# Later first casts, a later store and a later turn of the stream in the two MLPs of a hybrid decoder trunk

## Chip, cores and metric

One core of a Trainium2 chip runs the whole kernel. The metric is the device time of one launch in microseconds (us), the median of three runs. A profiled execution of the same program gives the rows below; its span runs from the first to the last instruction.

## What is computed

The reference is a decoder trunk of two layers on a stream x of 512 tokens with 1024 features, all in float32. Each layer adds an attention block and then an MLP to the stream. Cut to what matters here:

```
x = x + mixer(rms_norm(x, g_mix))                    # attention, one kind per layer
x = x + square(relu(rms_norm(x, g_ffn) @ w_up)) @ w_down
```

`w_up` is 1024 x 4096 and `w_down` 4096 x 1024. After layer 0 a shared compressed key/value is computed from the stream; after layer 1 a last RMS norm ends the trunk.

## The kernel before

Every float32 product is made of three TensorE matmuls: each operand is cut into a rounded part ("hi") and the rest ("lo"), and `three` (line 238) multiplies hi by hi, hi by lo and lo by hi. For a weight tile this costs a **cast** on ScalarE (`w_cast`, line 673) and a **low** subtraction on VectorE (`w_low`, line 683). The activations are cut the same way in `scaled` (line 260). The gain of the norm is multiplied in there; the norm's factor per token is computed apart and multiplied in at the end.

An MLP (`ffn`, line 631) is a list `seq` of products, one per step. The first eight steps are up products U0 to U7 (`up_mm`, line 709: 24 matmuls of 512 columns each into one bank of PSUM); from step 8 on up products alternate with down products (q1, q5, p6, x3 and so on). The up products have two PSUM banks (tag "up"). A bank comes free when `up_post` (line 721) has read it on ScalarE, so U2 cannot begin before `up_post(0)` has read U0.

The order of the work around a product is written by hand. `at(step, rank, fn)` (line 662) puts a piece of work into `due`; steps are emitted in order, and within one step by rank: 0 the product itself, 1 `up_post` of the product before, 3 a low, 6 a cast, 9 a load. While this runs (`order["on"]`, line 866) every instruction on TensorE, VectorE and ScalarE is chained to the one emitted before it on the same engine (lines 109 to 121), so that each of these three engines keeps the written order. SyncE, which issues the loads, is not chained: a scheduler at compile time places its instructions, and may issue a load earlier than written. Work emitted before the steps (the out projection, `scaled`, the store and the turn below) isn't chained either.

For the up product of step m the piece of weights is loaded at step m-8 (512 KB, line 700), cast at step m-5 and given its low at step m-4 (lines 840 to 842); steps below -8 count as -8. The raw pieces have only two buffers, so load 3 waits until the low of piece 1 has been taken, load 4 until that of piece 2, and so on. The weights of the down products come as "quads" (`quad`, line 702, 512 KB each), which have eight buffers of their own. The number of a cast, low or load below is that of its up product. Piece 0 is loaded and cut during the out projection.

Two things stand in step 0 beside U0. Behind its matmuls `rstd_of` (line 275) sums the squares on TensorE and starts the norm's factor: three short VectorE instructions (lines 286 to 289), then twelve on GpSimd. They have rank 0, being part of `up_mm(0)`. In layer 0 `rstd_tile` follows U2 (line 719): TensorE spreads the factor along the tokens and ScalarE copies it.

Before the steps of the MLP of layer 0 the stream (`x`, eight tiles of 256 KB) is stored to DRAM (lines 876 and 877), to be read again at its end. Before those of layer 1 `turn_stream` (line 1132) turns the stream into rows of tokens: 32 transposes on TensorE in eight units of four, and eight copies on ScalarE.

Of the kernel before, what the change touches and what calls it, by code (L numbers as in the profile page):

```python
# [17 lines left out]
P = 128  # L18
D = 1024
S = 512  # L20
NB = S // P
KD = D // P
# [31 lines left out]

PATTERN = "U U q1 U q5 U p6 U x3 U x2 U x4 U p7".split()
CLOSING_PATTERN = "U U q1 U U q5 U p6 U U x3 U x2 p7 x4".split()
V4_BEFORE = (5, 6)


# [13 lines left out]
def pieces():  # L73
# [3 lines left out]
    for p in range(1, FH // 2):  # L77
        out += [("v4", 1024)] * (2 * V4_BEFORE.count(p)) + [("qk", 1024)] * 2
    out += [("fo", 1024)] * 8
# [15 lines left out]
@with_exitstack  # L95
def trunk(ctx: ExitStack, tc: tile.TileContext, xT, wts, gains, fing, rope, out):
    real = tc.nc
    order = {"on": False, "last": {}}

    class Engine:  # L100

# [4 lines left out]
        def __getattr__(self, op):  # L106
            fn = getattr(self.engine, op)

            def call(*args, **kw):
                ins = fn(*args, **kw)  # L110
                if order["on"]:
                    before = order["last"].get(self.name)
                    if before is not None:
                        tc.add_manual_dep(
                            ins.ins,
                            before,
                            mybir.DependencyInfo(mybir.DependencyClass.NoSync, mybir.DependencyReason.DATA),
                            reason="as written",
                        )
                    order["last"][self.name] = ins.ins.name  # L120
                return ins

            return call

    class Core:
        tensor, vector, scalar = (Engine(n) for n in ("tensor", "vector", "scalar"))
        sync, gpsimd = real.sync, real.gpsimd

    nc = Core()

# [5 lines left out]
    keep = ctx.enter_context(tc.tile_pool(name="keep", bufs=1, space=bass.MemoryType.DRAM))  # L136
# [13 lines left out]
    def nm(s):  # L150
        uid[0] += 1
        return f"{s}{uid[0]}"

    def bank(tag, shape=(P, S)):
        return psum["pool"].tile(list(shape), F32, tag=tag, name=nm(tag), bufs=psum["tags"][tag])

    def rt(shape=(P, S)):
        return rp.tile(list(shape), F32R, tag="r", name=nm("r"))
# [4 lines left out]
    def f32(ap):  # L163
        return ap.bitcast(F32)
# [8 lines left out]
    ident = const.tile([P, P], F32, name="ident")  # L173
# [86 lines left out]
    def scaled(x, gname, k):  # L260
        hi, lo = rt(), rt()
        nc.scalar.activation(out=hi, in_=x, func=AF.Copy, scale=g(gname, k))
        nc.vector.scalar_tensor_tensor(out=lo, in0=x, scalar=g(gname, k), in1=f32(hi), op0=ALU.mult, op1=ALU.subtract)
        return hi, lo
# [162 lines left out]
    with ExitStack() as fx:  # L427
# [16 lines left out]
        acc = xs[0]  # L444
# [63 lines left out]
        for kp in range(4):  # L508
            whi, wlo = piece("v")
            for tb in range(NB):  # L510
                for k2 in range(2):
                    k = kp * 2 + k2
# [10 lines left out]
        def v4_gen(q):  # L523
            ws = [piece("v4"), piece("v4")]
            for tb in range(NB):
                pp = bank("acc")[:, :256]
                t = slice(tb * P, (tb + 1) * P)
                for k in range(KD):
                    whi, wlo = ws[k // 4]
                    c = slice(k % 4 * 256, k % 4 * 256 + 256)  # L530
                    three(pp, whi[:, c], wlo[:, c], h[k][0][:, t], h[k][1][:, t], k == 0, k == KD - 1, flip=True)
                    if k == 3:
                        yield 6
                value_parts(q, tb, pp)
                yield 6
# [54 lines left out]
        for p in range(1, FH // 2):  # L590
            for q in range(2):
                if V4_BEFORE[q] == p:
                    fill.add(("v4", q + 2), v4_gen(q + 2))
# [16 lines left out]
    def out_proj(name, ctxs, res, outs):  # L610

        acc = tt()
        for f in range(KD):
            xf = f32(rt())
            nc.sync.dma_start(xf, res[:, f, :])
            if f < len(outs):
                op, w = outs[f]
                three(op, *w[KD - 1], *ctxs[KD - 1], False, True)
            else:
                op = bank("acc")  # L620
                linear(op, piece(name), ctxs)
            nc.vector.tensor_tensor(xf, xf, op, op=ALU.add)
            square_sum(acc, xf, f == 0)
            x.append(xf)
        return acc

    x = []
    acc = out_proj("fo", [parts[k] for k in range(KD)], xT, outs)


    def ffn(acc, layer, tokens, tail, begin=None):

# [5 lines left out]
        with ExitStack() as fs:  # L640
            rawp = fs.enter_context(tc.tile_pool(name="mlp_raw", bufs=8, reuse_waits="tile"))
            sp = fs.enter_context(tc.tile_pool(name="mlp_s", bufs=4, reuse_waits="tile"))
            h = [scaled(x[k], gname, k) for k in range(KD)]
            if begin:
                begin()
            s, quads, s1, held, filled = {}, {}, {}, {}, set()
            norm = {}

# [2 lines left out]
            for c in range(CHUNKS):  # L651
                n = 8 * (c + 1)
                for what in CLOSING_PATTERN if c == CHUNKS - 1 else PATTERN:
                    if what == "U":
# [7 lines left out]
            def at(step, rank, fn, *args):  # L662
                due.setdefault(max(step, -8), []).append((rank, len(due.get(max(step, -8), [])), fn, args))
# [70 lines left out]
            def right(hf, kind):  # L734
                q = {f"B{a + 1}{b + 1}": quads.get((hf, a, b)) for a in range(2) for b in range(2)}
                return q["B11" if kind in ("T1", "T2", "T4") else "B12" if kind == "T3" else kind]
# [95 lines left out]
            for m, (what, n) in enumerate(seq):  # L832
                own = m % 2 == 0
                if what == "U":
                    if n == 0:
                        parts_ = state["ready"].pop(first)
                        los[0] = [tuple(t[:, j * S : (j + 1) * S] for t in parts_) for j in range(2)]
                    else:
                        src = lambda i=first + n: raws[i]
                        at(m - 8, 9, load, first + n)  # L840
                        at(m - 5, 6, w_cast, m, src, own)
                        at(m - 4, 3, w_low, m, src)
                    at(m, 0, up_mm, m, n)
                    at(m + 1, 1, up_post, n)
                    continue
                lk, rk = PRODUCTS[what]
                ready = max(posted[4 * n + j] for j in range(4))
                for key in {"q1": ["00"], "q5": ["01"], "p6": ["11"], "x2": ["10"]}.get(what, []):
                    at(m - 10, 9, quad, n, int(key[0]), int(key[1]))
                if rk[0] == "T":  # L850
                    at(m - 6, 4, right_sum, n, rk)
                if lk[0] == "S":
                    assert ready <= m - 4
                    at(max(m - 6, ready), 4.5, left_sum, n, lk)
                src = lambda n=n, rk=rk: right(n, rk)
                at(m - 5, 6, w_cast, m, src, own)
                at(m - 4, 3, w_low, m, src)
                assert ready <= m - 3
                at(max(m - 4, ready), 5, s_cast, m, n, lk)
                at(max(m - 3, ready + 1), 2, s_low, m, n, lk)  # L860
                at(m, 0, down_mm, m, what, n)
                if n % 2 and what[0] != "p":
                    at(m + 1, 1, down_post, what)
            tail(len(seq), max(posted.values()), at, locals())
            for step in sorted(due):
                order["on"] = True
                for _, _, fn, args in sorted(due[step], key=lambda d: d[:2]):
                    fn(*args)
            order["on"] = False
# [3 lines left out]

    stage("mlp0", up=2, go=2, keep=4)
    xmid = keep.tile([P, KD, S], F32, name="xmid")
    for k in range(KD):
        nc.sync.dma_start(xmid[:, k, :], x[k])
    xkeep = keep.tile([P, KD, S], F32, name="xkeep")
    ytok = [[f32(rt()) for _ in range(2)] for _ in range(NB)]
    xnew, hk, hm = {}, {}, {}  # L880
# [66 lines left out]
            for b in range(2):  # L947
                at(e + j // 2, 4, combine, b, part)

    ffn(acc, 0, ytok, by_features)  # L950
    for f in range(4, KD):
        close_feature(f)
    acc = closing["acc"]
# [10 lines left out]
    with ExitStack() as mx:  # L964
# [44 lines left out]
        for part in range(2):  # L1009
            for n in range(3):  # L1010
                w = blocks(piece("ka"))
                for m in range(2):
                    q = 2 * n + m
                    for j in range(4):
                        k = 4 * part + j
# [104 lines left out]
    x = []  # L1120
    acc = out_proj("mo", ctxs, xkeep, outs)
# [4 lines left out]
    xtok = [[f32(rt()) for _ in range(2)] for _ in range(NB)]  # L1126
# [2 lines left out]
    nc.scalar.dma_start(gfin, fing.partition_broadcast(P))  # L1129
    sums = fpool.tile([P, 2, NB], F32, name="sums")  # L1130

    def turn_stream():
        for tb in range(NB):
            for o in range(2):
                pp = bank("keep")
                for j in range(4):
                    nc.tensor.transpose(pp[:, j * P : (j + 1) * P], x[4 * o + j][:, tb * P : (tb + 1) * P], ident)
                nc.scalar.copy(xtok[tb][o], pp)

    def half_sum(tb, o):  # L1140
        junk = tt()
# [75 lines left out]
def _cols(w, lo, n):  # L1217
    return _blk(w, slice(lo, lo + n))


def _pack(i):
# [7 lines left out]
    for p in range(1, 8):  # L1229
        for q in range(2):  # L1230
            if V4_BEFORE[q] == p:
                b = _cols(fw, 2 * W + (q + 2) * 256, 256)
# [82 lines left out]
```

## Time and profile before

| | us |
|---|---|
| median of three runs | 1160.76 |
| the three runs | 1160.25, 1160.76, 1166.07 |
| the profiled execution's own time | 1166.28 |
| its span | 1164.5 |
| TensorE matmul busy in the span | 1128.8 |

The span is 1.8 us shorter than the profiled execution's own time. The MLP of layer 0 begins at about 262 us of the span and that of layer 1 at about 808 us. Nearly every instruction carries line 110, the helper that chains the engines, so groups are told apart by tiles: `up` is the bank of an up product, `go` that of the norm's sums, `keep` that of a transpose, `raw` a loaded piece of up weights, `q` a quad, `rs` the norm's factor, `s` the output of `up_post`, `whi`, `wlo` and `r` cut weights or activations. "[5.58 <-ACT s]" behind an instruction says that its engine was idle for 5.58 us before it and that an instruction of ScalarE writing `s` ended this.

### The profile page before, as it was taken

The page shows a single profiled execution, that of the slowest core. Times are in us where ns is not written, and L with a number is a line of the kernel's source. Part 1 is how long each engine was busy: PE and PEld are TensorE (multiplying, and loading weights), DVE is VectorE, ACT ScalarE, POOL GpSimd, SP SyncE. Part 2 cuts the span into 40 slices and gives each one's busy share as a digit, 9 for nine tenths or more (in the row PEclk, how much of TensorE's full clock was granted, in tenths as well). Part 3 has the DMA queues.
Part 4 walks back from the last instruction along what each step waited for, and adds up shares of the span by engine and source line. Part 5 has one row for each costly group of instructions (what it writes and reads, how often), then busy time and mean ns, then how long its engine had stood idle before and what let it go on. Part 6 is the DMA issues. An engine that isn't in the chain of part 4 may idle for free.

```text
span 1164.5 us, 14272 instructions
## 1 busy us (share of the span) xinstructions
PE 1128.8 (97%) x5356; PEld 922.3 (79%) x5356; DVE 783.0 (67%) x1413; ACT 574.4 (49%) x1053; POOL 22.4 (2%) x86
## 2 busy tenths in 40 slices
PE   8999999997999999999999899999899999999996
PEld 6777887786888888888887768788688888888875
DVE  6797888773457676677893678836346666765775
ACT  5555655554455454444353466626446444445611
POOL 1000000001000000000000100000100000000000
PEclk9999999998999999999999889999899999999998
DMA  5422222185204315211342121315511512511301
GB/s 184 128 101 80 74 91 73 37 281 206 73 37 154 99 43 192 74 55 64 119 167 91 34 64 50 109 55 191 189 37 54 181 57 71 184 64 41 127 1 73
DMA packets 36565, 116.65 MB, mean 100 GB/s; under 512 B 4224, under 2 KB 4864, under 8 KB 36496
## 3 DMA queue, kind: packets, MB, share of 16 engines
q1 hardware_dynamic: 35888, 114.15, 30.0%
q8 instruction: 42, 0.69, 0.3%
q0 software_dynamic: 320, 1.05, 0.2%
q10 hardware_dynamic: 288, 0.55, 0.2%
q14 instruction: 27, 0.22, 0.1%
HBM read 109.40 MB, written 6.32 MB: 99 GB/s over the span
## 4 chain that ended last, share of the span: by engine, by line
PE 90%; DMA 3%; DVE 3%; ACT 2%; issue 1%; POOL 1%; SPq 0%; POOLq 0%; ACTq 0%
PE up L110 32%; PE acc L110 20%; PE go L110 17%; PE sc L110 8%; PE tp L110 7%; PE keep L110 6%; DMA raw<-wts 2%; DVE r L110 1%; ACT r L110 1%; DVE wlo L110 1%; DMA q<-wts 1%; DMA nb<-csc 0%; DMA t<-xT 0%; DVE t L110 0%; DVE sl L110 0%
## 5 line engine op out<-in xcount | busy, mean ns | idle before, releaser
L110 PE MATMUL acc<-r,whi 128*128 128x512 f32 x600 | 196.2, 407 | 5.3 <-ACT whi L110 4.9
L110 PE MATMUL up<-r,r 128*128 128x512 f32 x808 | 192.4, 390 | 1.2 <-ACT s L110 1.2
L110 PE MATMUL up<-r,whi 128*128 128x512 f32 x544 | 173.7, 396 | 10.2 <-ACT s L110 10.2
L110 PEld LDWEIGHTS up<-r,r 128*128 128x128 f32 x808 | 151.4, 188 | 33.1 <-ACT s L110 1.4
L110 DVE TENSOR_TENSOR t<-s,t 128x512 fp32r<-128x512 f32 x84 | 57.8, 688 | 128.8 <-ACT t L110 128.7
L110 DVE TENSOR_TENSOR wlo<-raw,whi 128x1024 fp32r<-128x1024 f32 (+3 forms) x95 | 111.3, 1171 | 42.5 <-ACT whi L110 42.3
L110 ACT CAST whi<-raw 128x1024 fp32r<-128x1024 f32 (+3 forms) x95 | 95.5, 1008 | 86.6 <-PE acc L110 28.7
L110 PEld LDWEIGHTS acc<-r,whi 128*128 128x128 f32 x600 | 111.2, 192 | 31.1 <-ACT whi L110 4.9
L110 ACT ACTIVATE s<-up 128x512 f32<-128x512 f32 x56 | 33.4, 597 | 198.3 <-PE up L110 198.3
L110 PEld LDWEIGHTS up<-r,whi 128*128 128x128 f32 x544 | 103.7, 191 | 32.5 <-ACT s L110 11.1
L110 PE MATMUL acc<-r,wlo 128*128 128x512 f32 x300 | 119.2, 397 | 0.0
L110 PE MATMUL up<-r,wlo 128*128 128x512 f32 x288 | 113.3, 393 | 0.0
L110 PE MATMUL go<-r,t 128*128 128x512 f32 x360 | 86.5, 389 | 0.0
L110 PE MATMUL sc<-r,r 128*128 128x512 f32 (+6 forms) x480 | 81.5, 360 | 2.0 <-ACT r L110 1.6
L110 PE MATMUL go<-whi,t 128*128 128x512 f32 x240 | 78.7, 389 | 0.0
L110 PEld LDWEIGHTS go<-r,t 128*128 128x128 f32 x360 | 67.6, 188 | 14.0
L110 PEld LDWEIGHTS sc<-r,r 64*128 64x128 f32 (+1 forms) x480 | 55.9, 188 | 25.8 <-issue 10.3
L110 ACT ACTIVATE t<-t,sm 128x512 f32<-128x512 f32 (+3 forms) x96 | 53.3, 557 | 36.7 <-DVE sm L110 36.2
L110 DVE TENSOR_TENSOR r<-raw,r 128x512 fp32r<-128x512 f32 x72 | 46.5, 685 | 33.9 <-ACT r L110 33.9
L110 PEld LDWEIGHTS acc<-r,wlo 128*128 128x128 f32 x300 | 57.4, 191 | 12.8 <-issue 0.4
L110 DVE TENSOR_TENSOR wlo<-q,whi 128x1024 fp32r<-128x1024 f32 x45 | 54.9, 1221 | 16.7 <-ACT whi L110 16.3
L110 PEld LDWEIGHTS up<-r,wlo 128*128 128x128 f32 x288 | 55.0, 191 | 11.6
(180 smaller groups left out, 1869.4 us busy)
## 6 DMA issues: line engine op xcount, KB each, us to landing
raw<-wts SPq DMA_DIRECT2D x122, 512.0 KB, 3.5
q<-wts SPq DMA_DIRECT2D x56, 512.0 KB, 4.5
nb<-csc SPq DMA_DIRECT2D x8, 512.0 KB, 4.8
t<-xT SPq DMA_DIRECT2D x8, 256.0 KB, 5.9
r<-xT SPq DMA_DIRECT2D x8, 256.0 KB, 5.6
xmid<-r SPq DMA_DIRECT2D x8, 256.0 KB, 5.4
r<-xmid SPq DMA_DIRECT2D x8, 256.0 KB, 4.4
xkeep<-r SPq DMA_DIRECT2D x8, 256.0 KB, 2.3
```

The lines of the kernel that those rows point to most:

```text
L110: ins = fn(*args, **kw)
```

## The change

Three edits. The casts of the up products of steps 1 to 9 move to later steps by the table `BEGIN`: for m = 1 to 9 the cast stands at steps -1, -1, 0, 1, 2, 3, 4, 4, 5 (before: -4, -3, -2, -1, 0, 1, 2, 3, 4), and each low one step after its cast. The store of the stream in layer 0 moves into steps 1 to 4 (two tiles each, rank 9.5, behind the loads of the step). The turn of layer 1 moves into steps 1 to 8 (one unit each behind the step's product, its copy one step later). SyncE is chained in the written order for all steps below 9.

```
+BEGIN = (0, -1, -1, 0, 1, 2, 3, 4, 4, 5)
...
-                if order["on"]:
+                if order["on"] and (self.name != "sync" or order["loads"]):
...
-        tensor, vector, scalar = (Engine(n) for n in ("tensor", "vector", "scalar"))
-        sync, gpsimd = real.sync, real.gpsimd
+        tensor, vector, scalar, sync = (Engine(n) for n in ("tensor", "vector", "scalar", "sync"))
+        gpsimd = real.gpsimd
...
-            if begin:
-                begin()
...
+                        cast = max(m - 5, min(m - 2, BEGIN[m])) if m < len(BEGIN) else m - 5
                         at(m - 8, 9, load, first + n)
-                        at(m - 5, 6, w_cast, m, src, own)
-                        at(m - 4, 3, w_low, m, src)
+                        at(cast, 6, w_cast, m, src, own)
+                        at(cast + 1, 3, w_low, m, src)
...
+            begin(at)
             tail(len(seq), max(posted.values()), at, locals())
             for step in sorted(due):
-                order["on"] = True
+                order["on"], order["loads"] = True, step < 9
...
-    for k in range(KD):
-        nc.sync.dma_start(xmid[:, k, :], x[k])
+    def put_away(at):
+        for k in range(KD):
+            at(1 + k // 2, 9.5, lambda k: nc.sync.dma_start(xmid[:, k, :], xold[k]), k)
...
-    def turn_stream():
-        for tb in range(NB):
-            for o in range(2):
-                pp = bank("keep")
...
+    def turn_stream(at):
+        turned = {}
...
+        for n, (o, tb) in enumerate((o, tb) for o in range(2) for tb in range(NB)):
+            at(1 + n, 0.5, turn, tb, o)
+            at(2 + n, 1.5, lambda tb, o: nc.scalar.copy(xtok[tb][o], turned[tb, o]), tb, o)
```

## Rows read from the trace of the kernel before

**Rows 1.** The page's first part: busy time, share and instructions of each engine.
```profile
PE 1128.8 (97%) x5356; PEld 922.3 (79%) x5356; DVE 783.0 (67%) x1413; ACT 574.4 (49%) x1053; POOL 22.4 (2%) x86
```

**Rows 2.** Busy time by stretch, layer 0: length, engines, granted clock, DMA share, GB/s.
```profile
274.20:279.80 5.60, 0.03 (x1) 0.03 (x1) 2.90 (x7) 2.29 (x5) 3.85 (x12) 0.69 0.56 186
279.80:283.30 3.50, 3.50 (x9) 2.78 (x10) 1.45 (x2) 1.62 (x2) 0.48 (x2) 0.52 0.56 155
...
287.00:289.20 2.20, 1.02 (x10) 0.83 (x8) 0.00 (x0) 1.17 (x3) 0.00 (x0) 1.00 0.00 0
```

**Rows 3.** The same view, beginning of the MLP of layer 1.
```profile
823.50:828.10 4.60, 0.02 (x1) 0.02 (x1) 1.05 (x3) 1.67 (x4) 2.02 (x11) 0.76 0.58 214
```

**Rows 4.** Timeline of TensorE, layer 0: start, duration, instruction, idle before.
```profile
267.63 0.95 PE L110 MATMUL go<-ones,t 128*128 128x1 f32 x8
268.44 5.75 PE L110 MATMUL up<-r,r 128*128 128x512 f32 x24
279.77 1.22 PE L110 MATMUL up<-r,whi 128*128 128x512 f32 x2 [5.58 <-ACT s L110]
...
286.91 1.05 PE L110 MATMUL go<-ident,rs 128*128 128x128 f32 x8
289.13 5.74 PE L110 MATMUL up<-r,r 128*128 128x512 f32 x24 [1.18 <-ACT s L110]
```

**Rows 5.** Timeline of TensorE, beginning of the MLP of layer 1.
```profile
807.65 2.15 PE L110 MATMUL keep<-ident,r 128*128 128x128 f32 x16
...
810.58 1.91 PE L110 MATMUL keep<-ident,r 128*128 128x128 f32 x16
...
828.08 1.22 PE L110 MATMUL up<-r,whi 128*128 128x512 f32 x2 [4.63 <-ACT s L110]
...
835.78 5.60 PE L110 MATMUL up<-r,r 128*128 128x512 f32 x24
```

**Rows 6.** The chain that ended last, layer 0: start, duration, what.
```profile
266.38 6.09 DMA raw<-wts
...
273.19 1.29 DVE r L110 x2
...
274.51 3.55 DMA raw<-wts
...
278.08 1.14 ACT r L110 x2
```

**Rows 7.** The same chain at the beginning of the MLP of layer 1.
```profile
815.57 3.70 DMA raw<-wts
...
821.27 5.11 DMA raw<-wts
```

**Rows 8.** The chain of the whole span: an up product in the steady stretch.
```profile
332.95 5.44 PE up L110 x24
```

**Rows 9.** Timeline of VectorE, layer 0: the start of the norm's factor.
```profile
274.40 0.15 DVE L110 TENSOR_SCALAR rs<-go 128x4 f32<-128x4 f32 x1
274.59 0.38 DVE L110 TENSOR_SCALAR rs<-rs 128x4 int32<-128x4 int32 x2
```

**Rows 10.** Busy time by stretch: while load 3 was under way, and a steady stretch.
```profile
264.00:270.40 6.40, 6.40 (x34) 5.41 (x33) 3.57 (x5) 2.44 (x4) 0.00 (x0) 1.00 1.01 394
...
300.00:320.00 20.00, 20.00 (x90) 16.57 (x89) 9.25 (x12) 9.90 (x16) 0.00 (x0) 1.00 0.14 45
```

**Rows 11.** Timelines of ScalarE and VectorE, layer 1: copies of the turn, last low activations.
```profile
809.73 3.97 ACT L110 COPY r<-keep 128x512 f32<-128x512 f32 x8
...
809.86 0.75 DVE L110 SCALAR_TENSOR_TENSOR r<-r,gsb,r 128x512 fp32r<-128x512 f32 x1
```

**Rows 12.** TensorE in the attention of layer 1: a stop, and the stretch after it.
```profile
676.93 0.73 PE L110 MATMUL sc<-r,r 128*128 128x512 f32 x2 [1.26 <-ACT r L110]
...
678.00:680.00 2.00, 2.00 (x6) 0.92 (x6) 0.98 (x3) 1.80 (x4) 0.00 (x0) 0.77 0.78 222
```

More of the change, by code (lines that the diff above doesn't have):

```diff
@@ L97, in trunk @@
     real = tc.nc
-    order = {"on": False, "last": {}}
+    order = {"on": False, "loads": False, "last": {}}
     class Engine:
@@ L628, in trunk, with ffn @@
     acc = out_proj("fo", [parts[k] for k in range(KD)], xT, outs)
-    def ffn(acc, layer, tokens, tail, begin=None):
+    def ffn(acc, layer, tokens, tail, begin):
         gname = f"ffn{layer}"
@@ L875, in trunk @@
     xmid = keep.tile([P, KD, S], F32, name="xmid")
-    for k in range(KD):
-        nc.sync.dma_start(xmid[:, k, :], x[k])
+    xold = x
+    def put_away(at):
+        for k in range(KD):
+            at(1 + k // 2, 9.5, lambda k: nc.sync.dma_start(xmid[:, k, :], xold[k]), k)
     xkeep = keep.tile([P, KD, S], F32, name="xkeep")
@@ L948, in by_features @@
                 at(e + j // 2, 4, combine, b, part)
-    ffn(acc, 0, ytok, by_features)
+    ffn(acc, 0, ytok, by_features, put_away)
     for f in range(4, KD):
@@ L1130, in trunk, with turn @@
     sums = fpool.tile([P, 2, NB], F32, name="sums")
-    def turn_stream():
-        for tb in range(NB):
-            for o in range(2):
-                pp = bank("keep")
-                for j in range(4):
-                    nc.tensor.transpose(pp[:, j * P : (j + 1) * P], x[4 * o + j][:, tb * P : (tb + 1) * P], ident)
-                nc.scalar.copy(xtok[tb][o], pp)
+    def turn_stream(at):
+        turned = {}
+        def turn(tb, o):
+            turned[tb, o] = bank("keep")
+            for j in range(4):
+                nc.tensor.transpose(turned[tb, o][:, j * P : (j + 1) * P], x[4 * o + j][:, tb * P : (tb + 1) * P], ident)
+        for n, (o, tb) in enumerate((o, tb) for o in range(2) for tb in range(NB)):
+            at(1 + n, 0.5, turn, tb, o)
+            at(2 + n, 1.5, lambda tb, o: nc.scalar.copy(xtok[tb][o], turned[tb, o]), tb, o)
     def half_sum(tb, o):
```

## Prediction

> **What bounds the kernel now.** First the page's busy times: TensorE is busy for 97% of the span [rows 1], so only what lets it stop, or slows it, can matter. Next the busy time by stretch. At the beginning of each MLP stands a stretch in which TensorE does almost nothing: 0.03 of 5.60 us in layer 0 [rows 2] and 0.02 of 4.60 us in layer 1 [rows 3], and in both the granted clock falls, to 0.52 in the 3.5 us after the stop in layer 0 (1.2 GHz instead of 2.4). The timelines of TensorE give the end of each stop: idle for 5.58 and 4.63 us, until ScalarE writes `s`, which is `up_post(0)` [rows 4, 5]. So U2 waits for the bank of U0. The chain says why `up_post(0)` is late: load 3 lands, low 3 is taken, load 5 goes out at 274.51 and takes 3.55 us, cast 5 follows at 278.08 [rows 6]. Cast 5 stands in step 0 and `up_post(0)` in step 1, so on ScalarE the reader of a full bank stands behind a cast whose weights aren't there, weights that TensorE wants three products later. In layer 1 load 5 goes out at 821.27 and takes 5.11 us [rows 7].
>
> What this costs, slow clock included: U2 of layer 0 takes from 279.77 to 286.91, 7.14 us [rows 4] against 5.44 [rows 8]: 1.70 us on top of 5.58. U2 of layer 1 takes 828.08 to 835.78, 7.70 us [rows 5]: 2.26 on top of 4.63. Together 14.2 us, about the most that the edit of the casts can bring back.
>
> **The change, part by part: the casts.** Now only cast 3 stands ahead of `up_post(0)`, not cast 5. But a second order changes with it. Lows 1 and 2 now stand in step 0 with rank 3, and the three VectorE instructions that start the norm's factor stand in step 0 with rank 0. So these go first, and they wait for `rstd_of`, which TensorE does after U0. The trace shows that this order binds: the sums of layer 0 were done at 267.63 + 0.95 = 268.58 [rows 4], yet the first of the three ran at 274.40 [rows 9], right behind low 3 [rows 6]. After the change it is the lows that stand behind: low 1, needed by the third matmul of U1, and behind that low load 3 (two raw buffers), cast 3, `up_post(0)` and U2.
>
> Layer 0, from 268.58. The three instructions take 274.59 + 0.38 - 274.40 = 0.57 us [rows 9]; low 1 takes 1.29 for two halves [rows 6], 0.65 for the first: it is there at 269.80, and with a weight load the third matmul starts at about 270.0. Without a wait it would start at 268.44 + 2 x 5.44/24 = 268.9. A new stop in U1: 1.1 us. U1 ends at 268.44 + 5.44 + 1.1 = 274.98. Low 1 is whole at 270.44, load 3 goes out then (before: 266.38). Its landing is the unknown: 6.09 us before [rows 6], with the DMA engines full (share 1.01, 394 GB/s [rows 10]); 3.55 for load 5 later. I take 3.55, since the stores and six quads that filled those engines are now written behind it (only two quads, of steps 12 and 13, stay unchained and may still be early). It lands at 274.0. From landing to the start of U2 were 279.77 - 278.06 = 1.71 us (cast, read of the bank), so U2 starts at 275.7, 0.7 late; with 6.09 it would be 3.3 late. U2 at full clock takes 5.44, and from its end to U3 pass 289.13 - 286.91 = 2.22 us as before (`rstd_tile` and its copy [rows 4]; the twelve GpSimd instructions took 3.85 us busy [rows 2] and are over by then). U3 starts at 283.4 instead of 289.13: **5.7 us**.
>
> Layer 1. U0 starts where the 32 transposes started, 807.65 [rows 5]; its last block needs the last low activations, there at 809.86 + 0.75 = 810.6 [rows 11], while that block comes 7/8 of 5.44 us later, at 812.4. U1 follows 5.44 + 0.81 later (0.81 is 268.44 - 267.63), at 813.9; the sums end at 814.04; low 1 by the same terms: first half at 815.26, a stop of 1.1, U1 ends at 820.4, its unit of transposes (1.91/4 = 0.48 [rows 5]) at 820.9. Load 3 out at 815.9, 3.70 as before [rows 7] (bound above: 5.11), U2 1.71 behind: 821.3, 0.4 late (1.8). U2 and its unit 5.92: U3 at 827.3 instead of 835.78, gross 8.5. Six units of transposes are still to come, 2.9 us. Net **5.6 us**.
>
> **The lower bound of the stop in U1.** If a low that is ready were not held, nothing of the 1.1, 0.7 and 0.4 would stay: U3 at 281.5 and 825.7, gains of 7.6 and 7.1.
>
> **The store.** Eight issues move past loads 1 to 9 and six quads on SyncE's queue. Nobody waits for them until the end of the MLP except the ring of buffers that the stream occupies. It's written behind load 9, which waits for low 7 in step 5; cast 9 there wants room in the ring. At 394 GB/s [rows 10] load 9, a quad and two tiles (1.5 MB) need 4 us, and ScalarE may be late by a step, since U7 needs `up_post(5)` only one product later. I take nothing, with the cost of a step's delay as a rival.
>
> **The quads.** Chaining SyncE keeps them out of the out projection. They now follow loads 8 and 9, and are used from step 5 on; the steady stretch uses 0.14 of the DMA engines [rows 10]. Nothing for them.
>
> **The turn.** The transposes cost the same on TensorE, four behind each of eight products; they had hidden no wait, as TensorE ran through them, so only the place changes. The eight copies (0.5 us each, 3.97 for all [rows 11]) leave the time before cast 1 and join steps 2 to 9, in which ScalarE is busy for half the time (9.90 of 20 us [rows 10]).
>
> **Sum.** 5.7 + 5.6 = 11.3 us. The profiled execution took 1166.28 us, so it would take 1155.0; the median of the three runs lies 5.5 us below that execution, and the same difference from the median gives 1149.5. I forecast that.
>
> **A page of the notes against a term.** The landing of load 3 is taken from rows, at 3.55 and 3.70 us. The Trainium skill's page "DMA: Bandwidth & Descriptors" (Anatomy of one DMA) fits a single transfer, on GpSimd's path, as 2.0 us plus its bytes over 436 GB/s. An estimate by it for 512 KB is 3.2 us, and the sum would be 12.1 us instead of 11.3. The trace differs, its shortest of the four loads being 3.55, and I keep that.
>
> **Rivals.**
> - *No hold* (0.08): VectorE takes the lows first after all. Gain 7.6 + 7.1 = 14.7, 1146.1 us. Against it stands the late start of the factor in the trace.
> - *The clock falls all the same* (0.15): U1, U2 and U3 of layer 0 each begin or go on after a stop of about 1 us. For it: in the attention of layer 1 a stop of 1.26 us was followed by a stretch at a granted clock of 0.77, with TensorE busy throughout [rows 12]. Against it: the stretch with the stop of 1.18 us ahead of U3 kept 1.00 [rows 2, 4]. Price: 1.7 + 2.3 as now, gain 7.3, 1153.5 us. The Trainium skill's "TensorE: Matmul & The Clock Gate" (HAM oscillation) says that waits between matmuls bring the half clock back again and again; by that rule this case is the likely one, and the trace has shown both outcomes.
> - *Load 3 stays slow* (0.08): 6.09 and 5.11 us cost 2.5 + 1.4 of the gain: 7.4, 1153.4 us.
> - *The stop only moves* (0.08): slow load and slow clock together, so cast 3 does what cast 5 did: gain 3.4, 1157.4 us. The change then doesn't do what it says.
> - *Slower* (0.04): in steps 9 to 17 cast after cast comes late, since six quads and loads 8 to 11 stand on one chained queue behind each other and behind the stores. Each late cast holds an `up_post` or a down product. From 0.7 us in each of these sixteen or so products of both MLPs the gain is gone; with 1.75 us they lose 28, 1177 us. Against it: 0.14 DMA share there, and casts with four or five steps of lead.
>
> **How the numbers follow.** The forecast has what is left, 0.57; with clock or landing a little off it spans 1147 to 1152. The range for all goes from the case without hold, 1145.5, to short of the moved stop, 1156. A measurement can tell 0.5%, 5.8 us, from no change. Forecast, no hold, slow clock and slow load lie beyond that, 0.88; the last two by under 2 us, and the runs before spread by 5.8, so I put faster at 0.80, same at 0.15, slower at 0.05.
>
> **What would show it.** In the profile after, TensorE's long stops ahead of U2 should be gone, the clock at 1.00 through both beginnings. U1 should have a stop of about 1 us inside it, released by VectorE's low; that low should stand right behind the three instructions of the factor. U2 should be released by ScalarE again, under 1 us late. U3 of layer 0 should start some 6 us earlier. Four transposes should follow each of eight products of layer 1. The forecast is wrong if TensorE stops in steps 4 to 17, or if the clock shows 0.5 near U2.

## Result and the profile after

The changed kernel takes 1154.92 us in the median of ten runs (1149.63 to 1158.91), the kernel before 1163.73 in ten on the same chips (1158.94 to 1167.37): a ratio of 0.9919, 95% interval 0.9898 to 0.994. By the ratio that is 9.4 us less (7 to 12); 11.3 were forecast. The three runs shown ahead of the prediction had a median 3.0 us below that of the ten, and this, with the smaller gain, is why the forecast of 1149.5 us lies below the measured median.

The profiled execution of the changed kernel took 1152.35 us, its span 1150.6, 13.9 less than before. The page's busy times first, as in [rows 1] (a helper's line moved from 110 to 111):

```profile
PE 1122.5 (98%) x5356; PEld 916.1 (80%) x5356; DVE 783.1 (68%) x1413; ACT 574.6 (50%) x1053; POOL 24.0 (2%) x86
```

The busy time of matmuls fell by 6.3 us although none was taken out: fewer of them, in the beginnings and elsewhere, ran at the lower clock. The busy time by stretch over the beginnings of both MLPs, with columns as in [rows 2], then the stretch in which load 3 was under way before [rows 10]:

```profile
260.00:300.00 40.00, 37.63 (x171) 30.61 (x170) 15.39 (x22) 18.35 (x29) 4.14 (x13) 1.00 0.47 148
800.00:840.00 40.00, 39.01 (x185) 31.91 (x184) 15.69 (x23) 22.61 (x37) 4.14 (x13) 1.00 0.55 197
...
264.00:270.40 6.40, 5.72 (x30) 4.55 (x29) 2.86 (x7) 1.74 (x3) 1.56 (x3) 1.00 0.00 0
```

The granted clock is 1.00 in all three, where it had fallen to 0.52 before, and in the last of them the DMA engines, full before, are empty. The timeline of TensorE at the beginning of layer 0, answering to [rows 4]:

```profile
267.84 0.72 PE L111 MATMUL up<-r,r 128*128 128x512 f32 x2
...
269.25 5.29 PE L111 MATMUL up<-r,r 128*128 128x512 f32 x22 [0.68 <-DVE r L111]
275.04 0.73 PE L111 MATMUL up<-r,whi 128*128 128x512 f32 x2 [0.51 <-ACT s L111]
...
282.87 5.74 PE L111 MATMUL up<-r,r 128*128 128x512 f32 x24 [1.18 <-ACT s L111]
```

In place of one stop of 5.58 us there are two short ones: inside U1, released by VectorE, and ahead of U2, released by ScalarE. The stop of 1.18 us ahead of U3 is as before. A stop counts from the modelled end of the last matmul, which lies behind the moment at which the next one could have started. By starts, the third matmul of U1 comes 0.95 us late (269.25 against 267.84 + 0.46), and U2 starts 0.81 us later than 24 matmuls (5.44 us) and these 0.95 explain (275.04 - 267.84 - 6.39). The timeline of VectorE shows who holds it:

```profile
268.02 0.16 DVE L111 TENSOR_SCALAR rs<-go 128x4 f32<-128x4 f32 x1 [3.47 <-PE go L111]
268.21 0.37 DVE L111 TENSOR_SCALAR rs<-rs 128x4 int32<-128x4 int32 x2
268.50 1.29 DVE L111 TENSOR_TENSOR r<-raw,r 128x512 fp32r<-128x512 f32 x2
```

VectorE was idle for 3.47 us until the sums of U0 were done, and low 1 ran right behind the three instructions of the norm's factor. The chain that ended last, from there:

```profile
269.82 3.46 DMA raw<-wts
...
273.36 1.14 ACT r L111 x2
274.50 0.50 ACT s L111
...
275.04 5.76 PE up L111 x24
```

Load 3, cast 3, `up_post(0)`, U2: the chain of before without low 3, load 5 and cast 5. Layer 1, answering to [rows 5]:

```profile
805.74 0.72 PE L111 MATMUL up<-r,r 128*128 128x512 f32 x2
...
807.14 5.29 PE L111 MATMUL up<-r,r 128*128 128x512 f32 x22 [0.68 <-DVE r L111]
...
813.18 0.73 PE L111 MATMUL up<-r,whi 128*128 128x512 f32 x2 [0.30 <-ACT s L111]
819.11 5.71 PE L111 MATMUL up<-r,r 128*128 128x512 f32 x24
```

For a comparison that leaves out what happens elsewhere in the span I take the time from the start of U1 to that of U3. In layer 0 it was 20.69 us (268.44 to 289.13 [rows 4]) and is 15.03: 5.66 less. In layer 1 U1 began before at

```profile
817.71 5.75 PE L110 MATMUL up<-r,r 128*128 128x512 f32 x24
```

and U3 at 835.78 [rows 5]: 18.07 us. Now it is 13.37, and that holds two units of transposes (0.48 each) which stood ahead of U1 before: 5.66 less again. So 11.3 of the 13.9 us come from the two beginnings. The rest is outside them. One place is the attention of layer 1, in which the change edits nothing; busy time by stretch, before and after:

```profile
620.00:700.00 80.00, 74.01 (x331) 57.39 (x330) 48.97 (x96) 38.06 (x72) 7.45 (x36) 0.89 0.17 52
```
```profile
620.00:700.00 80.00, 73.33 (x350) 57.19 (x349) 54.23 (x119) 43.50 (x87) 8.58 (x36) 0.94 0.15 45
```

The granted clock there was 0.89 in one execution and 0.94 in the other. The experiments and the last section come back to this.

### The profile page after: what moved, and what is told of

The parts are those of the page before. It is cut to its first block, busy times and chain, and to the rows that moved or that the text cites. A ratio compares the mean times of both kernels' runs of the same rounds, so it can differ in the third digit from the quotient of the medians.

```text
span 1150.6 us, 14300 instructions
## 1 busy us (share of the span) xinstructions
PE 1122.5 (98%) x5356; PEld 916.1 (80%) x5356; DVE 783.1 (68%) x1413; ACT 574.6 (50%) x1053; POOL 24.0 (2%) x86
## 4 chain that ended last, share of the span: by engine, by line
PE 92%; DVE 3%; DMA 2%; issue 1%; ACT 1%; POOL 1%; SPq 0%; POOLq 0%; ACTq 0%; DVEq 0%
PE up L111 33%; PE acc L111 20%; PE go L111 18%; PE sc L111 8%; PE tp L111 7%; PE keep L111 6%; DVE r L111 1%; DMA raw<-wts 1%; DVE wlo L111 1%; DVE t L111 1%; ACT r L111 1%; DMA t<-xT 0%; DMA nb<-csc 0%; DVE sl L111 0%; DVE rs L111 0%
## 5 line engine op out<-in xcount | busy, mean ns | idle before, releaser
L111 PE MATMUL up<-r,whi 128*128 128x512 f32 x544 | 170.8, 390 | 0.8 <-ACT s L111 0.8
L111 PEld LDWEIGHTS up<-r,wlo 128*128 128x128 f32 x288 | 54.1, 188 | 11.3
L111 DVE TENSOR_TENSOR r<-q,r 128x512 fp32r<-128x512 f32 x94 | 60.4, 684 | 0.0
```

## Experiments

The theory: the stop came from cast 5 standing ahead of `up_post(0)` on ScalarE, and the two short stops left come from the norm's factor standing ahead of low 1 on VectorE. The rival: the moves of the store, the turn and the loads, which empty the DMA engines, carry the change. Diffs are against the changed kernel. "Measured" gives the ratio to the kernel before, run in the same round, with its 95% interval, and the median time. Times from U1 to U3 stand in a table behind the experiments.

**The casts alone.** `put_away` and `turn_stream` are again those of the kernel before, ahead of the steps.

```
+            begin()
...
-            begin(at)
...
-                order["on"], order["loads"] = True, step < 9
+                order["on"] = True
...
```

> The new places of the casts and lows alone; the store and the turn stand before the steps and SyncE is free, as before the change. My theory (cast 5 ahead of up_post(0) was the stop): TensorE's stops of 5.58 and 4.63 us ahead of U2 are gone and the clock stays at 1.00 there. In layer 1 from the start of U1 to that of U3 about 12.5 us (18.1 before the change), in layer 0 up to 2.5 us more than in the changed kernel, if load 3 has to share the DMA engines with the stores and quads. Gain 8 to 11 us against the kernel before. Rival (the moves free the engines that the first weights need): load 3 takes over 6 us, a stop of 3 us or more stays ahead of U2 in layer 0, the clock falls in it, and the gain is under 6 us.

Measured: 0.9925 (0.9898 to 0.9952), 1155.59 us. The timeline of TensorE, layer 0; the stretch beside load 3; load 3 in the chain:

```profile
270.10 5.27 PE L111 MATMUL up<-r,r 128*128 128x512 f32 x22 [0.71 <-DVE r L111]
275.94 0.73 PE L111 MATMUL up<-r,whi 128*128 128x512 f32 x2 [0.57 <-ACT s L111]
...
283.75 5.74 PE L111 MATMUL up<-r,r 128*128 128x512 f32 x24 [1.18 <-ACT s L111]
```
```profile
264.00:270.40 6.40, 5.69 (x29) 4.57 (x28) 2.85 (x7) 2.57 (x4) 0.82 (x2) 1.00 0.82 293
```
```profile
270.68 3.50 DMA raw<-wts
```

The same stops as with the moves (in layer 1, where no transposes stand behind U1, that ahead of U2 is 0.70 us instead of 0.30). The DMA engines are still busy for 0.82 of the stretch, but load 3 goes out behind that traffic, since low 1 is held, and lands in 3.50 us all the same. The new places of the casts alone have the gain of the changed kernel, within the intervals (0.9919 and, in the run beside this one, 0.9905); by the medians that run was 2.5 us faster than this one, with times that overlap.

**The moves alone.**

```
-                        cast = max(m - 5, min(m - 2, BEGIN[m])) if m < len(BEGIN) else m - 5
+                        cast = m - 5
```

> The casts at their old places; store and turn in the steps and SyncE chained, as after the change. My theory: the stop ahead of U2 stays in both layers, since cast 5 stands ahead of up_post(0): 4 to 5 us in layer 1 with the clock falling as before; 3 us or a little more in layer 0, where load 3 lands up to 2.5 us sooner. Gain 0 to 4 us against the kernel before. Rival (the moves carry the change): stops under 2 us and a gain over 6 us.

Measured: 0.9963 (0.9942 to 0.9984), 1160.34 us; by the ratio 4.3 us less than before, just over the 0 to 4 expected, by the medians 3.1. TensorE ahead of U2 in layer 0 and in layer 1, and load 3 of layer 0 and load 5 of layer 1 in the chain:

```profile
277.29 1.22 PE L111 MATMUL up<-r,whi 128*128 128x512 f32 x2 [3.13 <-ACT s L111]
...
818.54 0.73 PE L111 MATMUL up<-r,whi 128*128 128x512 f32 x2 [2.81 <-ACT s L111]
```
```profile
266.36 3.66 DMA raw<-wts
...
812.99 3.84 DMA raw<-wts
```

The stop stays in both layers, shorter. Layer 0 is as expected: load 3 takes 3.66 us instead of 6.09 [rows 6], and the stop is 2.45 us shorter. For layer 1 I expected 4 to 5 us and missed: load 5 takes 3.84 us instead of 5.11 [rows 7], 1.3 of the 1.8 us, and a unit of transposes behind U1 fills most of the rest. So the moves do shorten loads, but most of what they gain lies inside the stop that the casts remove. From U1 to U3 of both layers, in the table below, the casts alone gain 10.7 us and the moves alone 4.9, both together 11.3 and not 15.6. The ratios of whole runs are too coarse to show this.

**Lows 1 and 2 ahead of the norm's factor.**

```
-                        at(cast + 1, 3, w_low, m, src)
+                        at(cast + 1, -1 if m < 3 else 3, w_low, m, src)
```

> The changed kernel with lows 1 and 2 ahead of the three VectorE instructions of the norm's factor in step 0. My theory (the rest of the stops comes from that order): no stop inside U1, load 3 out some 3 us earlier, no stop ahead of U2 in either layer; U3 starts 1.8 us earlier in layer 0 and 1.4 us earlier in layer 1, so 3 us less than the changed kernel. Rival 1 (the stop in U1 has another cause, or load 3 holds U2 anyway): no difference. Rival 2 (the factor becomes late): the spread of the norm's factor after U2 in layer 0 waits for GpSimd, a new stop of 1 us or more there.

Measured: 0.9895 (0.9867 to 0.9922), 1151.29 us. VectorE and then TensorE in layer 0:

```profile
265.19 1.29 DVE L111 TENSOR_TENSOR r<-raw,r 128x512 fp32r<-128x512 f32 x2
...
268.75 0.16 DVE L111 TENSOR_SCALAR rs<-go 128x4 f32<-128x4 f32 x1 [1.01 <-PE go L111]
```
```profile
268.57 5.75 PE L111 MATMUL up<-r,r 128*128 128x512 f32 x24
...
281.82 5.74 PE L111 MATMUL up<-r,r 128*128 128x512 f32 x24 [1.18 <-ACT s L111]
```

Low 1 starts 3.6 us ahead of the factor, U1's 24 matmuls are one piece again, and no stop is left ahead of U2. From U1 to U3 are 13.25 us in layer 0, 1.8 less, and 11.85 in layer 1 (with two units of transposes), 1.5 less. Both rivals fall. By the medians it is 1.8 us faster than the changed kernel in the next run, within the spread of both; the profile is what shows the 3.3 us.

**The changed kernel again.**

> The changed kernel once more, beside the others on the same chip: 8 to 12 us less than the kernel before. If its two short stops bring the clock down in some executions, this profile may show 0.5 at the beginnings of the MLPs; if the spread of its times has its cause elsewhere, the half clock lies in other stretches.

Measured: 0.9905 (0.9881 to 0.9928), 1153.06 us. The stretches of layer 0, of the attention, and of layer 1:

```profile
260.00:300.00 40.00, 37.44 (x171) 30.49 (x170) 15.94 (x23) 17.89 (x28) 4.14 (x13) 1.00 0.43 136
620.00:700.00 80.00, 73.08 (x352) 57.21 (x351) 53.70 (x114) 43.19 (x86) 8.58 (x36) 0.94 0.15 45
800.00:840.00 40.00, 39.14 (x186) 32.01 (x185) 15.31 (x22) 21.94 (x36) 4.14 (x13) 1.00 0.55 198
```

The short stops leave the clock at 1.00 here too; it falls in the attention.

**The copy of the factor one step later.** The edit of lows 1 and 2, and in layer 0 `rstd_tile` cut in two: `row_mm` spreads the factor on TensorE behind U2, `row_copy` copies it on ScalarE one step later.

```
-                if n == 2 and layer == 0:
-                    norm["row"] = rstd_tile(norm["rs"], "go")
...
+            if layer == 0:
+                at(2, 0.6, row_mm)
+                at(3, 2, row_copy)
```

> The kernel of the run before (lows 1 and 2 first), and in layer 0 the copy of the norm's factor along the tokens stands one step later on ScalarE, behind up_post(2). Theory: the stop of 1.18 us ahead of U3, which no kernel so far has lost, comes from up_post(1) standing behind that copy; it goes, and U3 starts 1.2 us sooner after U1 than with lows first alone: 13.3 us from U1 to U3 becomes 12.1. In all some 4 us less than the changed kernel. Rival: U3 then waits for something else (low 3, or the bank), and the 1.2 us stay.

Measured: 0.9853 (0.9829 to 0.9877), 1147.94 us, the fastest of all. TensorE in layer 0, and the two beginnings by stretch:

```profile
278.77 1.05 PE L111 MATMUL go<-ident,rs 128*128 128x128 f32 x8
279.57 5.72 PE L111 MATMUL up<-r,r 128*128 128x512 f32 x24
```
```profile
260.00:300.00 40.00, 40.00 (x186) 33.36 (x185) 17.30 (x26) 20.79 (x33) 4.26 (x13) 1.00 0.55 181
...
800.00:840.00 40.00, 40.00 (x191) 33.21 (x191) 17.27 (x25) 22.50 (x37) 4.30 (x13) 1.00 0.59 213
```

The stop of 1.18 us is gone, and TensorE is busy for all of both stretches. The interval lies below both that were measured for the changed kernel. By the ratios it is some 6 us faster than that kernel in the run above, where 4 were expected; the profile gives 4.7 us to the two beginnings.

**The same without the moves.** The edits of the last run on the kernel with the casts alone.

> The same kernel without the moves: store and turn stand before the steps, SyncE is free. If the moves bring nothing of their own, no difference from the run with them beyond the spread. Rival: with lows 1 and 2 first, load 3 goes out about 266.5 us, where stores and quads fill the DMA engines; it then takes 5 to 6 us instead of 3.6, and U2 of layer 0 stops for up to 0.5 us. If the moves matter for TensorE's order in layer 1, this one is slower by 1 us or more there.

Measured: 0.9876 (0.9851 to 0.99), 1151.0 us. In the two beginnings the moves bring nothing: from U1 to U3 of layer 0 are 11.83 us in both, of layer 1 10.9 with them and 11.0 without. The rival's half is true: load 3, out at 265.74 into the traffic, landed after 5.0 us. But cast 3 still came in time:

```profile
270.84 1.14 ACT L111 CAST r<-raw 128x512 fp32r<-128x512 f32 x2 [5.14 <-DMA raw<-wts]
```

`up_post(0)` has read the bank at 271.89 + 0.59, while U2 starts at 273.39, right behind U1.

The whole runs do differ, though: of five times with the moves four lie below all five without, 3.1 us by the medians. Of the 2.2 us between the two profiles (spans of 1148.7 and 1150.9), some 1.9 arise between U3 of layer 0 and the beginning of the MLP of layer 1. At 618.6 us both are still level; over 620 to 700 us, in the attention, which neither edits, the granted clock was 0.89 with the moves and 0.87 without. The mean granted clock of whole executions was 0.989 to 0.994 with and 0.988 to 0.990 without. Whether the moves bring this about stays open.

**One more cast ahead, and one less.** First cast 4 also ahead of `up_post(0)`:

```
-BEGIN = (0, -1, -1, 0, 1, 2, 3, 4, 4, 5)
+BEGIN = (0, -1, -1, 0, 0, 2, 3, 4, 4, 5)
```

> The changed kernel with cast 4 back in step 0, ahead of up_post(0): one step of one cast. Theory: load 4 can only go out when low 2 is taken, 1.2 us behind load 3; it lands about 4 us later, so the stop ahead of U2 in layer 0 grows from 0.5 to 0.7 us to 2 to 2.5 us, and in layer 1 from 0.2 to 0.3 us to about 2 us. Rival (ScalarE's order doesn't set it): the stops stay.

Then cast 3 behind it too:

```
-BEGIN = (0, -1, -1, 0, 1, 2, 3, 4, 4, 5)
+BEGIN = (0, -1, -1, 1, 1, 2, 3, 4, 4, 5)
```

> The changed kernel with cast 3 also behind up_post(0), in step 1. Theory: no cast is left ahead of up_post(0) that waits for a load, so the stop ahead of U2 goes in both layers (0.5 to 0.7 and 0.2 to 0.3 us), while the stop of 0.68 us inside U1 stays. A price may show at U3, whose weights come later: low 3 should be there some 4 us before U3. Rival: U2 is held by something else, and its stop stays.

One execution each, 1156.76 and 1155.61 us, too few to compare by time. With cast 4 ahead, TensorE in both layers, and the stretches behind the stops:

```profile
277.86 1.22 PE L111 MATMUL up<-r,whi 128*128 128x512 f32 x2 [2.65 <-ACT s L111]
...
815.98 0.73 PE L111 MATMUL up<-r,whi 128*128 128x512 f32 x2 [2.65 <-ACT s L111]
```
```profile
277.90:282.00 4.10, 4.10 (x12) 3.28 (x13) 0.66 (x1) 0.56 (x1) 0.00 (x0) 0.62 0.68 233
...
816.00:820.00 4.00, 4.00 (x11) 3.16 (x12) 1.93 (x3) 3.21 (x6) 0.00 (x0) 0.61 0.52 183
```

One cast, one step earlier: the stop grows to 2.65 us in both layers, somewhat over the 2 to 2.5 expected, and the clock falls, in layer 0 within the stop: the first two matmuls of U2 took 1.22 us there, against 0.73 in the changed kernel. U2 took 7.05 us (277.86 to 284.91) and 7.16 us (815.98 to 823.14) instead of 5.44. With cast 3 behind, layer 0:

```profile
269.09 5.29 PE L111 MATMUL up<-r,r 128*128 128x512 f32 x22 [0.69 <-DVE r L111]
...
281.88 5.74 PE L111 MATMUL up<-r,r 128*128 128x512 f32 x24 [1.18 <-ACT s L111]
```

No stop ahead of U2 in either layer; the stop inside U1 stays, at 0.69 us, and U3 pays nothing. So the stop ahead of U2 is set by when the last cast ahead of `up_post(0)` gets its weights: with low 1 held it is 2.65 us with cast 4, 0.2 to 0.7 with cast 3, nothing with neither. The number of casts alone doesn't set it: the kernel with the moves alone and the kernel before have the same casts ahead and differ by 2.45 us in layer 0, and with low 1 first cast 3 costs nothing. The stop inside U1 comes from the hold of low 1.

All runs together, from the start of U1 to that of U3, in us (layer 1 without its two units of transposes, 0.96, where they stand inside):

| kernel | layer 0 | layer 1 |
|---|---|---|
| before | 20.7 | 18.1 |
| moves alone | 18.3 | 15.6 |
| cast 4 ahead | 18.6 | 16.4 |
| casts alone | 15.1 | 13.0 |
| changed | 15.0 | 12.4 |
| cast 3 behind | 14.2 | 11.9 |
| lows first | 13.3 | 10.9 |
| lows first, copy late | 11.8 | 10.9 |
| the same without the moves | 11.8 | 11.0 |

## Why the prediction was right, point by point

- **The stop and its cause.** Shown. Taking casts 4 and 5 from ahead of `up_post(0)` brings the gain with or without the moves, and putting cast 4 back alone brings back a stop of 2.65 us in both layers.
- **The hold of low 1.** Shown by the run with lows first. The term was right in kind and a little large: 0.95 us late instead of 1.1. What follows from it ahead of U2 was a little small: by starts, as the sum counts, U2 is 0.81 us late in layer 0 and 0.6 in layer 1, against 0.7 and 0.4.
- **The sum.** 5.7 and 5.6 us forecast, 5.66 and 5.66 in the profile. That it meets to 0.1 us is in part luck: the errors of the two terms above have opposite signs. As a ratio 11.3 us are 0.990, inside both intervals measured for this kernel (0.9898 to 0.994 and 0.9881 to 0.9928).
- **The landing of load 3.** Right value, wrong reason. The step says that the stores and quads that filled the engines "are now written behind it", and the low end of the price rests on that. With stores and quads at their old places it landed in 3.50 us: held by low 1, it goes out after them. The moves shorten load 3 only where low 1 isn't held, and there, with the lows first, slack hides the 5.0 us that it takes without them.
- **The page against the row.** The estimate of 3.2 us from the Trainium skill's "DMA: Bandwidth & Descriptors" (Anatomy of one DMA) was not reached: load 3 took 3.46 us, though the engines had been empty from 264 us until it went out. The rows were the better price here; in the run with the copy late, where load 3 went out at 265.7, it took 3.3 us.
- **The store and the quads at no cost.** Right: TensorE was busy for 37.00 of 37.00 us from 283 us on and for 80.00 of 80.00 from 320 on, in layer 1 for 21.00 of 21.00 from 819 on and for 160.00 of 160.00 from 840 on, transposes included, so the rival that ends slower has no place left.
- **No hold, slow load.** Both fell with the rows above. The price of the first was good: the run with the lows first, which takes the hold away, is 7.4 and 7.2 us from U1 to U3 below the kernel before, against 7.6 and 7.1.
- **The clock.** The rival did not come true: 1.00 over both beginnings in both profiles of this kernel. It does fall at a stop of 2.65 us, after which U2 took 1.6 and 1.7 us more; the rival's price for the two layers was 1.7 and 2.3. The Trainium skill's "TensorE: Matmul & The Clock Gate" (HAM oscillation) tells of a loop that waits for a load at every tile and falls back to the half clock each time. The trace agrees for the stop of 2.65 us and not for those of 1.18 us and less here; to call the fall the likely case for such short stops was more than that section says. The length of a stop isn't all: before, in the attention, a stop of 1.26 us was followed by a granted clock of 0.77 [rows 12], with no longer one in the 26 us ahead of it. What makes the difference is not shown.
- **The time itself.** The forecast took the median of three runs as its base, 3.0 us below that of ten; this moved the number and not the gain. It left the measured median 1.1 us inside the upper end of the range.

## What to carry to other kernels

On engines that keep the written order, ask of every instruction that releases another engine what stands ahead of it and what that waits for: a cast made far ahead of its use stopped TensorE because the reader of a PSUM bank stood behind it. When such an order is mended, look for what has now moved behind something else: here the weights' low part fell behind three tiny instructions of the norm, and moving it back, with the copy of the factor one step later, took another 4.7 us from the two beginnings (3.2 and 1.5). Two edits that shorten the same wait don't add up.

## Not expected of the hardware

The granted clock in the attention of layer 1 differs between profiles, with no edit there: over 620 to 700 us of the span it was 0.89 before the change, 0.94 in two profiles of the changed kernel, and in the runs with cast 4 ahead and with cast 3 behind

```profile
620.00:700.00 80.00, 74.43 (x367) 58.19 (x366) 54.31 (x117) 44.24 (x87) 7.45 (x36) 0.98 0.17 52
```
```profile
620.00:700.00 80.00, 72.86 (x323) 56.29 (x322) 50.18 (x104) 39.90 (x78) 8.57 (x36) 0.87 0.14 45
```

0.98 and 0.87. From the start of U3 in layer 0 to that of U1 in layer 1 these two kernels take 519.0 us (287.14 to 806.18) and 527.6 (281.88 to 809.52), 8.6 us apart with the same products between. An estimate from the two rows accounts for it: means of 0.98 and 0.87 over 80 us are some 3 and 21 us at the lower of the clock's two levels, and 18 us more at half speed cost about 9. The 8.6 us are nearly the spread of the ten runs of the changed kernel, 9.3 us, and these follow the clock too: the mean granted clock of an execution was 0.996 in one of 1149.8 us and 0.989 in the four of 1158.4 to 1158.9 us. A kernel with short waits in one stage can so hide a gain of 5 us in another from a single run. Why the clock falls more in one execution than in the next was not tried.
